# Latent attention: matmuls kept in program order, two key tiles at a time, weight sums in two VectorE accumulators, a quotient by logarithm and exponential

## The chip, the cores and the metric

The kernel runs on 1 core of one Trainium2 chip. The metric is the device time of one execution in microseconds (us), lower is better; the number given is the median of the runs. Engines are named as in the profile: PE is TensorE, PEld its weight loads, DVE is VectorE, ACT is ScalarE, POOL is GpSimd, SP is SyncE, which issues the DMAs.

## What is computed

The reference is a backbone of two layers over 1024 latent tokens and 256 context tokens of width 1024. In each layer the tokens are projected, and three groups of heads mix them: gated linear attention, retention (these two are the "linear heads" below), and multi-head latent attention with 8 heads of 64 value columns. Then come an output projection, layer norms and a convolutional feed-forward block. What the change touches is the latent attention:

```python
def _mla_attend(qn, qr, kn, kr, v):
    s = (jnp.einsum('bqhd,bkhd->bhqk', qn, kn)
         + jnp.einsum('bqhr,bkr->bhqk', qr, kr)).astype(jnp.float32) * MLA_SCALE
    p = jax.nn.softmax(s, axis=-1).astype(v.dtype)
    return jnp.einsum('bhqk,bkhe->bqhe', p, v)
```

Latent tokens attend to all 1280 keys, context tokens (in the first layer alone) to the 256 context keys. All of it is float32; the scores are made of three products of rounded parts (fp32r).

## The kernel before

The kernel is written as Python generators whose steps are woven together, and a tile scheduler then sets each engine's order from the written order and the dependencies; what a generator writes next may so be placed later than another generator's step, or later than its own following step. In each layer `mla` (latent attention) is woven with `lin` (the linear heads, lines 545 to 822), in two stretches of the span; before them lies the input projection (`proj`), behind them `wout` and the feed-forward block.

Latent attention goes head by head. Keys lie on the partitions: for each of 10 key tiles of 128 keys (`kt`) and each half `i` of the 1024 latent queries, `products` (line 942) makes a score tile of 128 keys x 512 queries in a PSUM bank with three fp32r matmuls, and ScalarE writes its exponential to one half of a weight tile of 128x1024 (line 1026, buffer tag `w2`, seven buffers that the projections' split weights use too). Two tiles later `values` (line 948) multiplies: one matmul of 64 columns for each half of the queries, the first into partitions 0 to 63 of the bank "av", the second into 64 to 127, over all ten key tiles. The weights are float32, and a float32 matmul shows as two records in the trace.

The sums of the weights are made elementwise first: GpSimd adds tiles 1 to 6 into tile 0 (line 1037), VectorE tiles 8 and 9 into tile 7 (line 1035), and then tile 7's into tile 0 (line 1043). In the first layer there are also two small tiles for the context queries (line 1013). `quotient` copies the bank "av" away (line 955), sums the accumulator over the keys by a matmul with ones (line 959, again one matmul for each half), takes the reciprocal on VectorE (line 960) and multiplies (line 963). It is a generator too; `tail()` does one step of it.

Beside a head's products the next head is prepared, two steps for each score tile (`beside`): key and query projections (lines 903 and 906, key into partitions 0 to 63 and query into 64 to 127 of the same banks), rotations and values, and `maxima`: one matmul for each block of 128 queries against 512 or 256 keys (line 925) and a maximum over it on VectorE (line 926), through three PSUM banks.

```python
                    elif kt >= 2:
                        k = kt - 2
                        P = held[k]
                        values(h, k, P, 512, k == 9)
                        if k in (8, 9):
                            nc.vector.tensor_tensor(held[7][:], held[7][:], P[:], op=ALU.add)
                        elif 0 < k < 7:
                            nc.gpsimd.tensor_tensor(held[0][:], held[0][:], P[:], op=ALU.add)
```

The linear heads use all engines: in `gla_out` VectorE and GpSimd multiply tiles of 128x512 (lines 693 to 773; line 716 is GpSimd's), `lin_chunk_out` has matmuls of lines 643 and 647, and `lin_norm` ends each group of 256 tokens with two matmuls with a block of ones (lines 660 and 666). Line 195 loads the weights of the dense layers, lines 212 and 213 split them into two parts, line 323 multiplies with them.

## Time and profile before

| | us |
|---|---|
| median of 3 runs | 3635.89 (3632.38 to 3640.07) |
| the profiled execution | 3636.93 |
| its span, first to last instruction | 3635.2 |
| PE busy | 3471.4 |
| DVE busy | 2331.7 |
| ACT busy | 1410.1 |
| POOL busy | 561.8 |

The page gives busy time by engine, the same in 40 slices of the span, the chain of work that ended last, and groups of instructions by line with their busy time, mean length, and the idle time before them with what ended it. A matmul's end is modelled, so how long matmuls take is best read from the start of one row of the timeline to the start of the next. A "PEclk" of 1.00 is TensorE at its full granted clock.

### The profile page before, as it was taken

To read this page: it belongs to the slowest core of one execution; us is meant where nothing else is said; L and a number is where in the kernel's file an instruction comes from. 1 tells how busy PE (TensorE), PEld (TensorE's weight loads), DVE (VectorE), ACT (ScalarE), POOL (GpSimd) and SP (SyncE) were. 2 spreads that over 40 slices of the span, in tenths; PEclk is the share of its full clock that TensorE was granted. 3 is DMA by queue.
4 is the path that set the end of the run, shared out by engine and by line. 5 is a ranking of instruction groups with operands and counts; after the bars stand their busy time and mean duration, and the time that the engine had idled before them with its cause. 6 is when DMAs were issued, how large, how long until landed. Compare 5 with 4: busy or idle time off the path is not lost. (4 is left out here: it accounts for less than half of the span.)

```text
span 3635.2 us, 50748 instructions
## 1 busy us (share of the span) xinstructions
PE 3471.4 (95%) x20270; PEld 2749.7 (76%) x20270; DVE 2331.7 (64%) x3371; ACT 1410.1 (39%) x2355; POOL 561.8 (15%) x583
## 2 busy tenths in 40 slices
PE   8998999997999999999999999889999999999998
PEld 6995544443999999899999897444446788888897
DVE  4336678777676445675557734878776875577555
ACT  3333333333354332343334443333333554345433
POOL 0001454444011000000000000453441000000001
PEclk9998899998999999999999999899999999999999
DMA  8653011021322333432223444011114222323221
GB/s 293 199 175 112 26 31 46 30 82 63 126 72 99 118 118 130 156 103 78 76 76 115 154 132 138 23 35 38 33 48 155 93 93 93 97 90 116 94 95 51
DMA packets 174702, 354.63 MB, mean 98 GB/s; under 512 B 15648, under 2 KB 92912, under 8 KB 174464
## 3 DMA queue, kind: packets, MB, share of 16 engines
q1 hardware_dynamic: 174464, 351.38, 29.5%
q8 instruction: 159, 2.61, 0.3%
q14 instruction: 79, 0.65, 0.1%
HBM read 310.09 MB, written 36.51 MB: 95 GB/s over the span
## 5 line engine op out<-in xcount | busy, mean ns | idle before, releaser
L323 PE MATMUL ps<-h,w 128*128 128x320 f32 (+5 forms) x9600 | 1681.6, 336 | 27.5 <-ACT h L212 16.4
L323 PEld LDWEIGHTS ps<-h,w 128*128 128x128 f32 x9600 | 1539.6, 190 | 166.3 <-ACT h L212 18.7
L213 DVE TENSOR_TENSOR w<-ws,w 128x1024 fp32r<-128x1024 f32 x360 | 440.2, 1223 | 589.7 <-PE ps L323 289.1
L1188 PE MATMUL ps<-hid,w 128*128 128x256 f32 (+4 forms) x3696 | 576.3, 316 | 1.5 <-ACT hid L212 1.5
L1188 PEld LDWEIGHTS ps<-hid,w 128*128 128x128 f32 x3696 | 538.9, 189 | 35.9 <-issue 7.6
L212 ACT CAST w<-ws 128x1024 fp32r<-128x1024 f32 x360 | 379.1, 1054 | 415.4 <-PE ps L1188 290.9
L1026 ACT ACTIVATE w<-ps 128x512 f32<-128x512 f32 x320 | 188.7, 596 | 338.5 <-PE ps L942 332.4
L942 PE MATMUL ps<-h,h 96*128 96x512 f32 (+3 forms) x1008 | 318.7, 431 | 0.3 <-ACT w L1026 0.2
L942 PEld LDWEIGHTS ps<-h,h 96*128 96x128 f32 (+1 forms) x1008 | 183.3, 199 | 151.8 <-issue 92.2
L926 DVE TENSOR_REDUCE sm<-ps 128x1 f32<-128x512 f32 (+1 forms) x400 | 221.7, 585 | 92.2 <-PE ps L925 90.3
L1037 POOL TENSOR_TENSOR w<-w,w 128x1024 f32<-128x1024 f32 x96 | 238.7, 2487 | 271.1 <-PE ps L948 173.0
L948 PE MATMUL ps<-w,hid 128*64 128x512 f32 (+1 forms) x704 | 276.0, 614 | 0.3 <-ACT w L1005 0.3
L1145 POOL MEMSET u<- 128x1 f32 (+1 forms) x264 | 21.5, 103 | 1613.4 <-DVE t L1156 1486.7
L1155 DVE SCALAR_TENSOR_TENSOR t<-u,vec,t 128x642 f32<-128x642 f32 (+3 forms) x176 | 144.6, 822 | 183.8 <-ACT t L1154 183.6
L1149 ACT COPY u<-ps 128x512 f32<-128x512 f32 (+4 forms) x264 | 118.4, 483 | 316.3 <-PE ps L323 316.3
L1193 DVE SCALAR_TENSOR_TENSOR y<-ps,mod,y 128x320 f32<-128x320 f32 (+5 forms) x376 | 197.1, 558 | 68.5 <-PE ps L1188 68.0
L925 PE MATMUL ps<-h,h 96*128 96x512 f32 (+1 forms) x400 | 156.1, 440 | 34.5 <-DVE sm L926 25.3
L925 PEld LDWEIGHTS ps<-h,h 96*128 96x128 f32 x400 | 77.8, 206 | 126.5 <-DVE sm L926 66.6
L716 POOL TENSOR_TENSOR hid<-hid,hid 128x512 f32<-128x512 f32 x108 | 153.3, 1439 | 83.0 <-ACT hid L696 56.2
L1154 ACT ACTIVATE t<-u,vec 128x642 f32<-128x642 f32 (+3 forms) x176 | 153.7, 873 | 0.4
L1156 DVE SCALAR_TENSOR_TENSOR t<-u,vec,t 128x642 f32<-128x642 f32 (+3 forms) x176 | 144.3, 820 | 11.4
L212 ACT CAST hid<-t 128x642 fp32r<-128x642 f32 (+3 forms) x88 | 59.5, 676 | 204.8 <-DVE t L1160 204.8
(197 smaller groups left out, 3134.4 us busy)
## 6 DMA issues: line engine op xcount, KB each, us to landing
ws<-in_up_dram SPq DMA_DIRECT2D x176, 512.0 KB
ws<-in_down_dram SPq DMA_DIRECT2D x88, 512.0 KB
ws<-in_ada_dram SPq DMA_DIRECT2D x80, 512.0 KB
ws<-in_w_in_dram SPq DMA_DIRECT2D x48, 512.0 KB
ws<-in_w_out_dram SPq DMA_DIRECT2D x32, 512.0 KB
y<-in_ada_dram SPq DMA_DIRECT2D x16, 512.0 KB
ws<-in_w_v_dram SPq DMA_DIRECT2D x16, 512.0 KB
hid<-in_xT_dram SPq DMA_DIRECT2D x16, 320.0 KB
```

The lines of the kernel that those rows point to most:

```text
L212: self.nc.scalar.copy(hi, src)
L213: self.nc.vector.tensor_tensor(lo, src, hi.bitcast(F32), op=ALU.subtract)
L323: nc.tensor.matmul(ps[:, i, 0:n], w_[:, k, :], h[k][:, part, o:o + n], start=(k == 0 and q == 0), stop=(k == 7 and q == 2))
L925: nc.tensor.matmul(t, q0[0:96, 128 * qi:128 * qi + 128], k0[0:96, o:o + n], start=True, stop=True)
L926: nc.vector.tensor_reduce(mx[:, qi:qi + 1] if qi < 2 else part[:, qi - 2, j:j + 1], t, axis=AX.X, op=ALU.max)
L942: nc.tensor.matmul(t, Kt[h % 2][ka][0:rows, 128 * kt:128 * kt + 128], Q[h][qa][0:rows, c0:c0 + n], start=(x == 0), stop=(x == 2))
L948: nc.tensor.matmul(op[64 * i:64 * i + 64, 0:n], V[h // 2][kt // 5][:, kt % 5, r:r + 64], P[:, i], start=(kt == 0), stop=last, skip_group_c ...
L1026: nc.scalar.activation(held[kt][:, i], t, AF.Exp, scale=MSCALE)
L1037: nc.gpsimd.tensor_tensor(held[0][:], held[0][:], P[:], op=ALU.add)
L1154: nc.scalar.activation(v[:, 0:n], u[:, 1:1 + n], AF.Identity, scale=cw(j, 1), bias=self.vec[l][:, V_CB + j:V_CB + j + 1])
L1188: nc.tensor.matmul(pb[i][:, 0:n], w[w_][:, x, ms], p.hh[f0 + x][hp][:, o - 1:o - 1 + n], start=(x == 0 and q == 0), stop=(x == gn - 1 and ...
L1193: nc.vector.scalar_tensor_tensor(t, pb[i][:, o:o + n], self.md(l, 5, m, who), t, op0=ALU.mult, op1=ALU.add)
```

## The change

1. A helper `pin` ties every matmul of `mla` to the one written before it, without a semaphore, so that the scheduler keeps them in the order in which they are written. Matmuls of the linear heads may still be placed between them.
2. The loop over key tiles takes two at a time: the products and exponentials of tiles kt and kt+1 (four score tiles), one `tail()`, then the value matmuls of tiles kt-2 and kt-1, both tiles' four matmuls in a row.
3. All adds of weight tiles are on VectorE: tiles 1 to 4 into tile 0, tiles 6 to 9 into tile 5. The two accumulators are not added to each other; `quotient` sums both by matmuls that accumulate in one bank (and both context tiles likewise). GpSimd has no work in `mla` any more but one fill.
4. The reciprocal becomes exp(-ln x) on ScalarE, with a Newton step of two operations on VectorE, whose sign goes into the last multiply.

```diff
+        prev = [None]
+
+        def pin(x):
+
+            if prev[0] is not None:
+                self.tc.add_manual_dep(x.ins, prev[0].ins.name, mybir.DependencyInfo(mybir.DependencyClass.NoSync, mybir.DependencyReason.DATA),
+                                       reason="in order")
+            prev[0] = x
...
-                nc.tensor.matmul(t, Kt[h % 2][ka][0:rows, 128 * kt:128 * kt + 128], Q[h][qa][0:rows, c0:c0 + n], start=(x == 0), stop=(x == 2))
+                pin(nc.tensor.matmul(t, Kt[h % 2][ka][0:rows, 128 * kt:128 * kt + 128], Q[h][qa][0:rows, c0:c0 + n], start=(x == 0), stop=(x == 2)))
...
-        def quotient(h, c0, n, P):
+        def quotient(h, c0, n, sums):
...
             t = bank("pre")[:, 0:n]
+            for x, P in enumerate(sums):
+                for i in range(2):
+                    pin(nc.tensor.matmul(t[64 * i:64 * i + 64, :], self.ones[:, 0:64], P[:, i], start=(x == 0), stop=(x == len(sums) - 1),
+                                         skip_group_check=True))
+            sums.clear()
+            del P
+
+            nc.scalar.activation(rb[:], t, AF.Ln)
+            nc.scalar.activation(rb[:], rb[:], AF.Exp, scale=-1.0)
+            nc.vector.tensor_tensor(u[:], t, rb[:], op=ALU.mult)
+            nc.vector.scalar_tensor_tensor(rb[:], u[:], -2.0, rb[:], op0=ALU.add, op1=ALU.mult)
+            yield
             for i in range(2):
-                nc.tensor.matmul(t[64 * i:64 * i + 64, :], self.ones[:, 0:64], P[:, i], start=True, stop=True, skip_group_check=True)
-            nc.vector.reciprocal(rb[:], t)
-            yield
-            for i in range(2):
-                nc.vector.tensor_tensor(o[r:r + 64, c0 + n * i:c0 + n * i + n], ov[64 * i:64 * i + 64, :], rb[64 * i:64 * i + 64, :], op=ALU.mult)
+                hs = slice(64 * i, 64 * i + 64)
+                nc.vector.scalar_tensor_tensor(o[r:r + 64, c0 + n * i:c0 + n * i + n], ov[hs, :], -1.0, rb[hs, :], op0=ALU.mult, op1=ALU.mult)
...
-            for kt in range(12):
+            for kt in range(0, 12, 2):
                 if kt < 10:
-                    held[kt] = self.w2([128, 2, 512], F32)
...
+                    for k in (kt, kt + 1):
+                        held[k] = self.w2([128, 2, 512], F32)
+                        for i in range(2):
+                            t = bank("sc")
+                            products(h, k, CTX + 512 * i, t)
+                            nc.scalar.activation(held[k][:, i], t, AF.Exp, scale=MSCALE)
+                            beside()
+                            if k == kt or i == 0:
+                                yield
+                tail()
+                if kt >= 2:
+                    for k in (kt - 2, kt - 1):
                         P = held[k]
                         values(h, k, P, 512, k == 9)
-                        if k in (8, 9):
-                            nc.vector.tensor_tensor(held[7][:], held[7][:], P[:], op=ALU.add)
-                        elif 0 < k < 7:
-                            nc.gpsimd.tensor_tensor(held[0][:], held[0][:], P[:], op=ALU.add)
-                        if k not in (0, 7):
-                            del held[k]
+                        if k % 5:
+                            A = held[k // 5 * 5]
+                            nc.vector.tensor_tensor(A[:], A[:], P[:], op=ALU.add)
+                            del held[k], A
                         del P
...
-            nc.vector.tensor_tensor(held[0][:], held[0][:], held[7][:], op=ALU.add)
-            tails.append(quotient(h, CTX, 512, held[0]))
+            tails.append(quotient(h, CTX, 512, [held[0], held[5]]))
```

The order that the scheduler makes of it is seen at three places. The first is PE in the middle of a head of layer 0. Before (L948 are value matmuls, one row a half, L925 row maxima, L942 products):

```order
L948 MATMUL ps<-w_4243,hid_4002 64x512
L925 MATMUL ps<-h_2551,h_4121 128x256
L948 MATMUL ps<-w_4243,hid_4002 64x512
L942 MATMUL ps<-h_3720,h_2549 128x512
L925 MATMUL ps<-h_2551,h_4121 128x512
L942 MATMUL ps<-h_3721,h_2549 128x512
L942 MATMUL ps<-h_3720,h_2550 128x512
```

and now (L957 are value matmuls, L934 row maxima, L951 products, L739 a linear head's):

```order
L934 MATMUL ps<-h_2551,h_4136 128x512
L957 MATMUL ps<-w_4192,hid_4014 64x512 x2
L957 MATMUL ps<-w_4215,hid_4014 64x512 x2
L739 MATMUL ps<-hid_4287,hid_4171 32x128 x2
L951 MATMUL ps<-h_3725,h_2549 128x512
L951 MATMUL ps<-h_3726,h_2549 128x512
L951 MATMUL ps<-h_3725,h_2550 128x512
L934 MATMUL ps<-h_2551,h_4136 128x256
```

The two halves of a key tile, which a row maximum stood between, now stand together, and two tiles' in a row; a product's three matmuls stand together too.

The second is DVE at a quotient of layer 0, with the row maxima around it. Before (L960 the reciprocal, L963 the last multiply, L926 maxima):

```order
L960 RECIPROCAL t_5343<-ps 128x512
L926 TENSOR_REDUCE sm_5421<-ps 128x1
L963 TENSOR_TENSOR y_4951<-t_5342,t_5343 64x512 x2
```

and now (L976 and L977 the Newton step, L981 the last multiply, L935 maxima):

```order
L976 TENSOR_TENSOR t_5388<-ps,t_5387 128x512
L935 TENSOR_REDUCE sm_5471<-ps 128x1
L977 SCALAR_TENSOR_TENSOR t_5387<-t_5388,t_5387 128x512
```

The Newton step's first operation stands where the reciprocal stood, with maxima behind it, and it reads what ScalarE's two steps have made.

The third is PE at the end of layer 0's stretch. Before (L959 the column sums of the last head, L660 and L666 the norm of the last linear group, L323 the output projection):

```order
L660 MATMUL ps<-hid_6386,bones 128x512
L948 MATMUL ps<-w_6427,hid_5654 64x512
L666 MATMUL ps<-hid_6451,bones 128x512
L959 MATMUL ps<-w_6192,ones 64x512 x2
L323 MATMUL ps<-h_6536,w_6492 128x256
```

and now (L969 the column sums, L643 and L647 the last linear group's output):

```order
L969 MATMUL ps<-w_6262,ones 64x512 x2
L969 MATMUL ps<-w_6406,ones 64x512 x2
L643 MATMUL ps<-hid_6451,hid_6503 128x128 x2
L647 MATMUL ps<-hid_6496,u_6448 64x128 x2
...
L660 MATMUL ps<-hid_6458,bones 128x512
L666 MATMUL ps<-hid_6526,bones 128x512
L323 MATMUL ps<-h_6616,w_6572 128x256
```

The last head's sums, which stood behind the last linear group, now stand ahead of that group's end.

Counted over both stretches in these orders, the two programs differ on PE as follows:

| on PE, from the first matmul of attention to its last, both layers | before | now |
|---|---|---|
| value matmuls of 512 queries: pairs of neighbouring halves / with a half of another kind / lone halves | 82 / 3 / 153 | 150 / 1 / 19 |
| key and query projections: pairs and lone halves | 93 | 82 |
| column sums of 512 queries: pairs and lone halves | 19 | 32 |
| neighbours of different tile shape | 782 | 503 |

## Rows read from the trace of the kernel before

**Rows 1.** The page: the span, and PE's busy time, its share and its instructions.

```profile
span 3635.2 us, 50748 instructions
PE 3471.4 (95%) x20270; PEld 2749.7 (76%) x20270; DVE 2331.7 (64%) x3371; ACT 1410.1 (39%) x2355; POOL 561.8 (15%) x583
```

**Rows 2.** Attention stretches: length, busy PE, PEld, DVE, ACT, POOL; PEclk, DMA share, GB/s.

```profile
321.00:902.00 581.00, 521.25 (x2494) 259.61 (x2494) 448.84 (x640) 201.08 (x440) 248.31 (x149) 0.90 0.15 45
2261.00:2760.00 499.00, 458.11 (x2145) 226.76 (x2138) 390.38 (x532) 180.52 (x376) 224.46 (x130) 0.93 0.15 46
```

**Rows 3.** Timeline of PE in layer 0: start us, us, engine, line, operation, records.

```profile
604.17 1.10 PE L942 MATMUL ps<-h,h 96*128 96x512 f32 x4
605.11 0.28 PE L925 MATMUL ps<-h,h 96*128 96x256 f32 x1
605.22 0.39 PE L942 MATMUL ps<-h,h 96*128 96x512 f32 x1
605.54 1.07 PE L948 MATMUL ps<-w,hid 128*64 128x512 f32 x2
606.54 0.50 PE L925 MATMUL ps<-h,h 96*128 96x512 f32 x1
606.98 1.08 PE L948 MATMUL ps<-w,hid 128*64 128x512 f32 x4
607.99 0.51 PE L925 MATMUL ps<-h,h 96*128 96x512 f32 x1
```

**Rows 4.** Timeline of PE, 890 to 893 us.

```profile
890.44 1.93 PE L948 MATMUL ps<-w,hid 128*64 128x512 f32 x6
892.30 0.38 PE L643 MATMUL ps<-hid,hid 128*128 128x128 f32 x1
```

**Rows 5.** Value matmuls by shape: busy us, mean ns, idle before.

```profile
L948 PE MATMUL ps<-w,hid 128*64 128x512 f32 x640 | 267.3, 643 | 0.0
```

**Rows 6.** VectorE's groups, whole span; two by min/median/max ns.

```profile
L1035 DVE TENSOR_TENSOR w<-w,w 128x1024 f32<-128x1024 f32 x32 | 49.0, 1531 | 7.9 <-PE ps L948 7.1 <-issue 0.2
L1043 DVE TENSOR_TENSOR w<-w,w 128x1024 f32<-128x1024 f32 x16 | 20.4, 1276 | 0.2
L1043 DVE TENSOR_TENSOR w<-w,w x16: 1208/1216/2173, 425.0 to 2756.9; 128x1024 f32<-128x1024 f32 x16
L960 DVE RECIPROCAL t<-ps 128x512 f32<-128x512 f32 (+1 forms) x24 | 61.3, 2553 | 7.3 <-PE ps L959 7.1
L963 DVE TENSOR_TENSOR y<-t,t 64x512 f32<-64x512 f32 (+1 forms) x48 | 60.9, 1268 | 0.9
L963 DVE TENSOR_TENSOR y<-t,t x48: 274/690/2831, 376.5 to 2764.4; 64x512 f32<-64x512 f32 x32, 64x128 f32<-64x128 f32 x16
```

**Rows 7.** GpSimd's groups, whole span.

```profile
L1037 POOL TENSOR_TENSOR w<-w,w 128x1024 f32<-128x1024 f32 x96 | 238.7, 2487 | 271.1 <-PE ps L948 173.0 <-ACT w L1026 93.9
L716 POOL TENSOR_TENSOR hid<-hid,hid 128x512 f32<-128x512 f32 x108 | 153.3, 1439 | 83.0 <-ACT hid L696 56.2 <-PE ps L948 9.4 <-DVE hid L338 8.2
```

**Rows 8.** A logarithm or exponential of 128x512 on ScalarE.

```profile
L333 ACT ACTIVATE hid<-hid 128x512 f32<-128x512 f32 x18 | 11.3, 629 | 11.3 <-DVE hid L332 11.0
```

**Rows 9.** Weight loads waiting for maxima, layer 0, layer 1: us, times, longest.

```profile
PEld ps L925 <- DVE sm L926: 39.4, 45, 4.4
...
PEld ps L925 <- DVE sm L926: 27.2, 33, 2.9
```

**Rows 10.** Timeline of PE at the end of layer 0's stretch.

```profile
899.46 1.13 PE L666 MATMUL ps<-hid,bones 128*128 128x512 f32 x2 [2.15 <-ACT hid L663]
900.51 1.08 PE L959 MATMUL ps<-w,ones 128*64 128x512 f32 x4
```

**Rows 11.** Busy us in three short pieces, columns as in rows 2.

```profile
376.00:399.00 23.00, 20.93 (x126) 12.18 (x125) 18.11 (x30) 7.76 (x13) 20.66 (x13) 1.00 0.05 12
399.00:416.00 17.00, 14.35 (x63) 8.21 (x63) 5.99 (x16) 2.43 (x5) 4.76 (x3) 0.51 0.06 17
2280.00:2297.00 17.00, 9.20 (x80) 4.69 (x80) 14.73 (x37) 4.18 (x18) 5.72 (x5) 0.51 0.00 1
```

More of the change, by code (lines that the diff above doesn't have):

```diff
@@ L857, in prod_v @@
             for t_ in range(10):
-                nc.tensor.matmul(ps[:, 128 * t_:128 * t_ + 128], S.ckv[:, 128 * t_:128 * t_ + 128], wk[:, 1, 128 * p:128 * p + 128],
-                                 start=True, stop=True)
+                pin(nc.tensor.matmul(ps[:, 128 * t_:128 * t_ + 128], S.ckv[:, 128 * t_:128 * t_ + 128], wk[:, 1, 128 * p:128 * p + 128],
+                                 start=True, stop=True))
             for i in range(2):
@@ L869, in prod_qr @@
                 for kc in range(2):
-                    nc.tensor.matmul(t, wr[:, kc, 128 * x:128 * x + 128], S.cq[kc][:, o:o + n], start=(kc == 0), stop=(kc == 1))
+                    pin(nc.tensor.matmul(t, wr[:, kc, 128 * x:128 * x + 128], S.cq[kc][:, o:o + n], start=(kc == 0), stop=(kc == 1)))
                 nc.scalar.copy(raw[:, o:o + n].bitcast(F32), t)
@@ L876, in prod_qr @@
                 nc.sync.dma_start(si[:, 0:n], a["msin"][:, o:o + n])
-                nc.tensor.matmul(t, self.permm[:], r, start=True, stop=True)
+                pin(nc.tensor.matmul(t, self.permm[:], r, start=True, stop=True))
                 nc.vector.tensor_tensor(t2[:, 0:n], t, si[:, 0:n], op=ALU.mult)
@@ L924, in maxima @@
                     t = bank("pre")[:, 0:n]
-                    nc.tensor.matmul(t, q0[0:96, 128 * qi:128 * qi + 128], k0[0:96, o:o + n], start=True, stop=True)
+                    pin(nc.tensor.matmul(t, q0[0:96, 128 * qi:128 * qi + 128], k0[0:96, o:o + n], start=True, stop=True))
                     nc.vector.tensor_reduce(mx[:, qi:qi + 1] if qi < 2 else part[:, qi - 2, j:j + 1], t, axis=AX.X, op=ALU.max)
@@ L931, in maxima @@
             t, r = bank("pre"), self.dgt()
-            nc.tensor.matmul(t[0:n, 0:128], mx[:, 10 - n:10], self.ident[:], start=True, stop=True)
+            pin(nc.tensor.matmul(t[0:n, 0:128], mx[:, 10 - n:10], self.ident[:], start=True, stop=True))
             nc.scalar.activation(r[0:n, :], t[0:n, 0:128], AF.Copy, scale=-1.0)
@@ L947, in values @@
             for i in range(2):
-                nc.tensor.matmul(op[64 * i:64 * i + 64, 0:n], V[h // 2][kt // 5][:, kt % 5, r:r + 64], P[:, i], start=(kt == 0), stop=last,
-                                 skip_group_check=True)
-        def quotient(h, c0, n, P):
+                pin(nc.tensor.matmul(op[64 * i:64 * i + 64, 0:n], V[h // 2][kt // 5][:, kt % 5, r:r + 64], P[:, i], start=(kt == 0), stop=last,
+                                 skip_group_check=True))
+        def quotient(h, c0, n, sums):
             r = 64 * (h % 2)
-            o, ov, rb = ob[h // 2], self.tt([128, n]), self.tt([128, n])
+            o, ov, rb, u = ob[h // 2], self.tt([128, n]), self.tt([128, n]), self.tt([128, n])
             nc.scalar.copy(ov[:], self.pb("av")[:, 0:n])
@@ L1012, in mla @@
                     values(h, kt, P[kt], 128, kt == 1)
-                nc.vector.tensor_tensor(P[0][:], P[0][:], P[1][:], op=ALU.add)
-                tails.append(quotient(h, 0, 128, P[0]))
+                tails.append(quotient(h, 0, 128, P))
                 tail()
@@ L1018, in mla @@
             held = {}
-            for kt in range(12):
+            for kt in range(0, 12, 2):
                 if kt < 10:
-                    held[kt] = self.w2([128, 2, 512], F32)
-                for i in range(2):
-                    if kt < 10:
-                        t = bank("sc")
-                        products(h, kt, CTX + 512 * i, t)
-                        nc.scalar.activation(held[kt][:, i], t, AF.Exp, scale=MSCALE)
-                        beside()
-                    if i == 0:
-                        tail()
-                    elif kt >= 2:
-                        k = kt - 2
+                    for k in (kt, kt + 1):
[10 more added lines that the diff above has]
+                    for k in (kt - 2, kt - 1):
                         P = held[k]
                         values(h, k, P, 512, k == 9)
-                        if k in (8, 9):
-                            nc.vector.tensor_tensor(held[7][:], held[7][:], P[:], op=ALU.add)
-                        elif 0 < k < 7:
-                            nc.gpsimd.tensor_tensor(held[0][:], held[0][:], P[:], op=ALU.add)
-                        if k not in (0, 7):
-                            del held[k]
+                        if k % 5:
+                            A = held[k // 5 * 5]
+                            nc.vector.tensor_tensor(A[:], A[:], P[:], op=ALU.add)
+                            del held[k], A
                         del P
-                    if kt < 10:
-                        yield
-            nc.vector.tensor_tensor(held[0][:], held[0][:], held[7][:], op=ALU.add)
-            tails.append(quotient(h, CTX, 512, held[0]))
+                if kt < 10:
+                    yield
+            tails.append(quotient(h, CTX, 512, [held[0], held[5]]))
             tail()
```

7 lines of the change are left out of this document (4 added, 3 removed).

## The prediction

> **What bounds the kernel now.** I read the page first, then the busy times of the two latent-attention stretches, then the timeline of TensorE (PE) inside one, then the groups by line, and the waits last. The profiled execution took 3636.9 us, 1.0 us over the median of the runs (3635.9); its span is 3635.2. PE is busy for 95% of it [rows 1]. The change lives in two stretches, 321 to 902 and 2261 to 2760 us, 1080 us together. There PE is busy for 521.3 and 458.1 us, so 101 us are idle, and its mean granted clock is 0.90 and 0.93; VectorE (DVE) is busy for 448.8 and 390.4, that is 78% [rows 2]. So PE is the limit there, with VectorE close behind.
>
> But PE's busy time is not all needed. The weight-by-value product of a key tile is two matmuls of 64 output columns, one into each half of the partitions (two records each, since the type is fp32). The timeline shows four such records taking from 606.98 to 607.99, **1.01 us, and two records alone from 605.54 to 606.54, 1.00 us** [rows 3]. Two halves that stand next to each other thus run at the same time, and a half by itself costs as much as both. Something between the halves costs the whole second half, and the order of the program before (the first fragment of the change's section) puts a row maximum between them again and again.
>
> **Price of a step and of a change of shape.** I call "step" a pair that runs together, or a lone half. Six records in a row (a pair and a lone half) take from 890.44 to 892.30, 1.86 us [rows 4]; less the 1.00 of the first step, a further step costs 0.86. The first one costs 0.14 more, for leaving. Entering costs too: four products start 0.235 us apart (604.17 to 605.11), but from the last one to the value matmul it is 0.32 (605.22 to 605.54) [rows 3]. In and out cost 0.23, or **0.117 us a change of tile shape**.
>
> **PE, counted in the two orders.**
> - Values of 512 queries: before, 82 pairs, 3 pairs with a key projection, 153 lone halves, 238 steps. After, 151 pairs and 19 lone halves, 170. 68 x 0.86 = -58 us. The group's 267.3 us [rows 5] fit 238 steps of 0.86 to 1.01, with some at the half clock.
> - Key and query projections, now chained in the order written: 93 steps become 82; 11 x 0.86 = -9.
> - Column sums of the weights: each quotient now sums two accumulators, so 19 steps of 512 become 32, +11, and eight more pairs of 128 columns, a quarter each, +2.
> - Changes of shape between neighbours, all matmuls of the stretches counted: 782 become 503; 279 x 0.117 = -33.
>
> Together -87 us at the full clock. The stretches ran at 0.915 on average [rows 2], so **-95 us**. No engine hides this: it is work of the engine that is the limit.
>
> **VectorE.** It gets 128 adds of 128x1024 in place of 32 + 16 and eight of a quarter the size. One line of such adds has a median of 1.22 and a mean of 1.28, the other a mean of 1.53 [rows 6]. At 1.22 the 128 are +156, and those that go are 49.0 + 20.4 + 8 x 0.3 = -72. The reciprocals go, -61. The Newton step adds two operations a quotient: at 0.69 each for the sixteen wide quotients and 0.27 for the eight small (the last multiply's median and shortest, 512 and 128 columns), +26. The last multiply becomes a scalar_tensor_tensor of the same size, 0. Sum: +49. On the other side GpSimd (POOL) loses its 96 adds, 238.7 us [rows 7]. While POOL runs, VectorE slows: the last multiply has a median of 0.69 and a longest of 2.83; at 32 x 0.69 + 16 x 0.27 its 48 would take 26 us instead of 61 [rows 6]. That line alone gives back up to 35, though POOL's other work causes a share. The relief lies between 0 and 239; I take 50, nearest to the row that shows it. VectorE thus stays at about 838 us, in 1013 instead of 1080: 83% in place of 78%.
>
> Against this stands a rule of the Trainium skill (SBUF — State Buffer, Who interferes with whom): a VectorE operation with two SBUF inputs and a GpSimd one that reads SBUF exclude each other, and the loser waits for the whole instruction. By it each of the 80 further adds could wait out a POOL multiply. The trace agrees on the lock only in part: the adds now on VectorE lose 0.3 us on average [rows 6].
>
> In numbers from rows alone: 80 x 0.31 (1.53 less 1.22) is +25 us of VectorE, 80 x 1.44 [rows 7] is +115. I take the first as the bound, since it is the same operation at the same place.
>
> **ScalarE** gets 24 logarithms and 24 exponentials, 0.63 us for a wide one [rows 8], at most 30 us on an engine busy for 35% [rows 2]; the table loads stay as many as they were. They lie in the quotient's chain: VectorE's first multiply now waits for two ScalarE steps (about 1.3 us), with row maxima queued behind it (second fragment), where the reciprocal held the queue for 2.55 on average [rows 6]. I count 0, bounds -1 and +1 us a quotient, 24 us either way. **SyncE** issues the same transfers, in an order that moves only with the quotients. The buffers that hold weights are seven: at a head's start two old accumulators, the last pair and the first new pair fill six, so the third tile's exponentials wait for the old sums. Those stand behind the new head's first products; I count 0, and the cover gone it is one add and one step, 2 us a head.
>
> **What is late next.** PE waits for the row maxima, 39.4 and 27.2 us [rows 9]. With 17% of VectorE's time free instead of 22%, I let these 67 grow in that proportion: **+20 us**. And at the end of layer 0 the third fragment shows the sums ahead of the linear heads' last matmuls. Now this last piece, from its first matmul at 892.30 [rows 4] to the end of the norm's at 900.51 [rows 10], runs beside value matmuls; after, beside nothing: **+8 us**, bounds 0 and 8.
>
> Sum: -95 + 20 + 8 = -67; 3637 - 67 = **3570 us**.
>
> **The rivals.**
> - *The clock comes back as well.* At 0.90 and 0.93 PE loses 58 + 35 = 93 us to half-rate pieces: from 399 to 416 us the clock is 0.51 (the lower of its levels, 1.2 and 2.4 GHz), right behind 23 us at 1.00 in which PE was busy for 20.9 [rows 11]. A third of that gone, and no more waiting than now: 3637 - 95 + 8 - 31 = 3519, with the waiting 3539; say 3530. For it: fewer lone halves. Against: PE will wait on VectorE.
> - *VectorE becomes the limit.* No relief, every add at 1.53: 839 + 49 + 25 = 913 us. In its densest stretch it is busy 14.73 of 17 us, 87% [rows 11]; 913 / 0.87 = 1049, 31 saved, 8 lost: 3614.
> - *Nothing arrives.* The saved PE time falls where PE would wait anyway: 3637.
> - *Slower: adds ahead of maxima.* The 128 adds come in 80 batches, 48 of two. The chain keeps PE from passing a late maximum with a later matmul of attention. If an add isn't covered by the value matmuls issued with it (two pairs, 1.87 us), PE stands for it. 156 us of adds uncovered to three quarters is +117: 3637 - 95 + 8 + 117 = 3667. It decides from 56% uncovered (87 of 156). Against: 1.87 us of matmuls stand beside each batch of 2.44.
> - *Slower: whole waits.* Each of the 80 adds loses 1.44: 839 + 49 + 115 = 1003 us, / 0.87 = 1153, 73 over: 3710. The Trainium skill's rule on the shared port, above, read at its strongest, gives this; the 1.53 of a row speaks against.
>
> **How the numbers follow.** Forecast 0.55, clock 0.13, VectorE 0.18, nothing 0.05, adds ahead of maxima 0.06, whole waits 0.03. A measurement of this kernel can tell 0.2%, 7 us, from no change. Faster: 0.55 + 0.13 + 0.18 = 0.86; same 0.05; slower 0.09. The forecast's own spread is the 24 us of the quotients and the 28 of waiting and end, about 3540 to 3600; the range adds the clock below (3519) and VectorE above (3614): 3518 to 3620.
>
> **What would show it.** Right: the value group falls from 267 us to under 200, and records alone become rare; POOL's adds are gone; the last multiply has a median of 0.69 and a mean near it; the stretches come to about 550 and 465 us. Wrong in a step: PE's waits for maxima grow beyond 90 us; adds on VectorE with means of 1.5 or more; a mean clock under 0.90. The forecast is wrong altogether if pairs stand together in the trace and the stretches are as long as before.

## The result and the profile after

The changed kernel takes **3591.6 us** (median; 3587.6 to 3593.5), the kernel before beside it 3636.1 us. The ratio is 0.9876, with a 95% interval of 0.9859 to 0.9893: 44.6 us faster, where the prediction has 66. The profiled execution took 3592.4 us; the rest is read from it. First the page, for [rows 1]:

```profile
span 3590.7 us, 50954 instructions
...
PE 3398.0 (95%) x20366; PEld 2762.3 (77%) x20366; DVE 2288.0 (64%) x3467; ACT 1433.9 (40%) x2403; POOL 329.3 (9%) x487
```

Then the two attention stretches, with the columns of [rows 2]. The second starts 41 us earlier, since the first is shorter:

```profile
321.00:862.00 541.00, 470.29 (x2537) 260.04 (x2536) 416.88 (x681) 211.34 (x465) 131.98 (x99) 0.88 0.15 46
2220.00:2718.00 498.00, 432.43 (x2135) 236.82 (x2136) 376.73 (x578) 188.44 (x390) 108.58 (x82) 0.86 0.15 46
```

Layer 0 saves 40 us and **layer 1 saves 1**. There PE has 26 us less to do and stands 25 us longer (498.00 less 432.43 is 65.6, against 40.9 in [rows 2]). The granted clock has fallen in both stretches, not risen. VectorE, forecast at 838 us as before, is busy for 794 in the two.

The groups by line, shapes apart, which answer to [rows 5, 6] (L957 values, L1053 all adds, L981 the last multiplication, L976 and L977 the Newton step), and L750, a masked copy of a linear head that the change doesn't touch:

```profile
L957 PE MATMUL ps<-w,hid 128*64 128x512 f32 x640 | 177.1, 648 | 0.0
L1053 DVE TENSOR_TENSOR w<-w,w 128x1024 f32<-128x1024 f32 x128 | 176.8, 1382 | 24.2 <-PE ps L957 18.4 <-ACT w L1042 3.7
L981 DVE SCALAR_TENSOR_TENSOR y<-t,t 64x512 f32<-64x512 f32 x32 | 23.9, 746 | 0.5
L750 DVE COPY_PREDICATED t<-msk,hid 32x128 f32<-32x128 uint8 x72 | 21.3, 295 | 1.0
L977 DVE SCALAR_TENSOR_TENSOR t<-t,t 128x512 f32<-128x512 f32 x16 | 11.0, 688 | 0.1
L976 DVE TENSOR_TENSOR t<-ps,t 128x512 f32<-128x512 f32 x16 | 11.0, 687 | 10.3 <-PE ps L951 7.1 <-ACT t L975 3.1
```

The value group falls from 267.3 to 177.1 us: the pairs are there. The masked copies fall from 636 to 295 ns on average without having been changed. In the kernel before they were (mean; then shortest, median and longest):

```profile
L750 DVE COPY_PREDICATED t<-msk,hid 32x128 f32<-32x128 uint8 x72 | 45.8, 636 | 0.9
L750 DVE COPY_PREDICATED t<-msk,hid x72: 281/298/2422, 392.7 to 2702.4; 32x128 f32<-32x128 uint8 x72
```

Most of them were as short then as now; some stood for up to 2.1 us, nearly one add of GpSimd (2.49 us in [rows 7]). Now the longest takes 305 ns.

What PE waited for from 320 to 2830 us, both stretches within (us in total, times, longest). First the longest in the kernel before, the maxima; then the changed kernel. The maxima (L934 on L935) are one of several now; the transpose of a head's maxima (L941), the sums (L969) and the first maxima of a head (L934 on L922) are new at this size:

```profile
PE ps L925 <- DVE sm L926: 25.3, 22, 4.2
...
PE ps L934 <- DVE sm L935: 26.5, 22, 5.5
PE ps L941 <- DVE sm L937: 25.9, 12, 5.3
PE ps L969 <- DVE h L922: 16.4, 4, 8.6
PE ps L934 <- DVE h L922: 10.5, 6, 2.9
```

The longest of these, on the timeline of PE (start us, us, then the operation):

```profile
686.91 2.31 PE L915 MATMUL ps<-y,ws 128*64 128x512 f32 x7
689.15 1.08 PE L727 MATMUL ps<-hid,hid 128*32 128x256 f32 x24
698.86 3.68 PE L969 MATMUL ps<-w,ones 128*64 128x512 f32 x8 [8.63 <-DVE h L922]
```

and what VectorE does meanwhile:

```profile
687.16 2.06 DVE L1053 TENSOR_TENSOR w<-w,w 128x1024 f32<-128x1024 f32 x1
689.14 1.50 DVE L758 TENSOR_TENSOR hid<-u 128x256 f32<-128x256 f32 x1
690.56 2.28 DVE L1053 TENSOR_TENSOR w<-w,w 128x1024 f32<-128x1024 f32 x1
692.76 1.48 DVE L761 TENSOR_TENSOR hid<-hid,u 128x256 f32<-128x256 f32 x1
694.17 1.21 DVE L1053 TENSOR_TENSOR w<-w,w 128x1024 f32<-128x1024 f32 x1
695.30 1.54 DVE L922 TENSOR_TENSOR h<-ps,h 64x1024 fp32r<-64x1024 f32 x2
...
697.58 1.57 DVE L922 TENSOR_TENSOR h<-ps,h 64x1024 fp32r<-64x1024 f32 x2
```

K and Q of the next head have just been multiplied (L915). The sums need a bank that the subtractions (L922) must empty first, and these stand behind three adds of weights and two steps of a linear head. Two of the adds take 2.06 and 2.28 us, the third 1.21, in a stretch in which GpSimd works for the linear heads (3.92 of the first 4 us, 3.96 of the next 9, below). In the chain nothing of attention may pass the sums. So PE stands for 8.63 us, and starts again at a lower clock (third piece; columns of [rows 2]):

```profile
686.00:690.00 4.00, 4.00 (x38) 1.79 (x34) 4.00 (x3) 0.56 (x2) 3.92 (x3) 1.00 0.04 11
690.00:699.00 9.00, 0.36 (x12) 0.14 (x4) 8.92 (x10) 3.39 (x6) 3.96 (x3) 0.72 0.00 0
699.00:715.00 16.00, 15.86 (x85) 9.47 (x86) 13.35 (x27) 9.29 (x23) 7.63 (x7) 0.84 0.07 18
```

### The profile page after: what moved, and what is told of

It reads as the page before. It is cut to its first block, busy times and chain, and to the rows that moved or that the text cites. A ratio compares the mean times of both kernels' runs of the same rounds, so it can differ in the third digit from the quotient of the medians.

```text
span 3590.7 us, 50954 instructions
## 1 busy us (share of the span) xinstructions
PE 3398.0 (95%) x20366; PEld 2762.3 (77%) x20366; DVE 2288.0 (64%) x3467; ACT 1433.9 (40%) x2403; POOL 329.3 (9%) x487
## 5 line engine op out<-in xcount | busy, mean ns | idle before, releaser
L323 PE MATMUL ps<-h,w 128*128 128x320 f32 (+5 forms) x9600 | 1676.0, 335 | 21.4 <-ACT h L212 12.6
L323 PEld LDWEIGHTS ps<-h,w 128*128 128x128 f32 x9600 | 1535.5, 190 | 158.3 <-ACT h L212 14.8
L951 PE MATMUL ps<-h,h 96*128 96x512 f32 (+3 forms) x1008 | 317.3, 436 | 3.8 <-DMA h<-mx 2.3
L951 PEld LDWEIGHTS ps<-h,h 96*128 96x128 f32 (+1 forms) x1008 | 189.5, 205 | 107.9 <-issue 70.2
L935 DVE TENSOR_REDUCE sm<-ps 128x1 f32<-128x512 f32 (+1 forms) x400 | 222.9, 588 | 52.3 <-PE ps L934 50.2
L934 PE MATMUL ps<-h,h 96*128 96x512 f32 (+1 forms) x400 | 153.3, 442 | 50.5 <-DVE sm L935 26.5
L1053 DVE TENSOR_TENSOR w<-w,w 128x1024 f32<-128x1024 f32 x128 | 176.8, 1382 | 24.2 <-PE ps L957 18.4
L957 PE MATMUL ps<-w,hid 128*64 128x512 f32 (+1 forms) x704 | 183.7, 618 | 0.0
L716 POOL TENSOR_TENSOR hid<-hid,hid 128x512 f32<-128x512 f32 x108 | 160.6, 1505 | 137.9 <-ACT hid L696 75.3
L934 PEld LDWEIGHTS ps<-h,h 96*128 96x128 f32 x400 | 84.2, 217 | 99.9 <-DVE sm L935 48.9
```

What stands on the lines that cost most here:

```text
L323: nc.tensor.matmul(ps[:, i, 0:n], w_[:, k, :], h[k][:, part, o:o + n], start=(k == 0 and q == 0), stop=(k == 7 and q == 2))
L716: nc.gpsimd.tensor_tensor(X[n][:], blk(E[n][:, 0, cs[i]]), qx[:], op=ALU.mult)
L934: pin(nc.tensor.matmul(t, q0[0:96, 128 * qi:128 * qi + 128], k0[0:96, o:o + n], start=True, stop=True))
L935: nc.vector.tensor_reduce(mx[:, qi:qi + 1] if qi < 2 else part[:, qi - 2, j:j + 1], t, axis=AX.X, op=ALU.max)
L951: pin(nc.tensor.matmul(t, Kt[h % 2][ka][0:rows, 128 * kt:128 * kt + 128], Q[h][qa][0:rows, c0:c0 + n], start=(x == 0), stop=(x == 2)))
L957: pin(nc.tensor.matmul(op[64 * i:64 * i + 64, 0:n], V[h // 2][kt // 5][:, kt % 5, r:r + 64], P[:, i], start=(kt == 0), stop=last, skip_gro ...
```

## The experiments

One table first. Steps (of the wide value matmuls) and changes of shape are counted in each order as ahead of the prediction. The four columns behind them are the two stretches together, from the row of the stretches: PE busy, PE idle (length less busy), VectorE busy, and what the clock loses (one less the granted clock, times the length). The column "time" is the median of the runs, and the last one its difference from the kernel before as timed beside it. The change was timed beside 3636 us, all others beside 3631 to 3632; so a difference from the change comes out some 4 us apart by the two columns (the text below takes the times).

| kernel | steps | shape changes | PE busy | PE idle | VectorE | clock | time | against before |
|---|---|---|---|---|---|---|---|---|
| before | 238 | 782 | 979 | 101 | 839 | 93 | 3636 | |
| the change | 170 | 503 | 903 | 136 | 794 | 135 | 3592 | -45 |
| before + chain | 173 | 583 | 947 | 193 | 841 | 182 | 3693 | +60 |
| before + pairs, no chain | 160 | 645 | 925 | 123 | 840 | 137 | 3617 | -15 |
| before + quotient | 230 | 763 | 975 | 99 | 816 | 110 | 3624 | -6 |
| before + adds | 242 | 789 | 964 | 59 | 817 | 67 | 3584 | -47 |
| before + adds + quotient | 242 | 789 | 957 | 51 | 793 | 61 | 3561 | -70 |
| before + adds + quotient + two tiles (the change, no chain) | 219 | 662 | 920 | 51 | 786 | 64 | 3523 | -109 |
| the change, no chain, pairs | 160 | 585 | 850 | 68 | 797 | 57 | **3467** | -165 |
| the change, half the adds on GpSimd | 172 | 512 | 916 | 171 | 804 | 153 | 3640 | +8 |
| the change, reciprocal | 171 | 492 | 922 | 155 | 830 | 148 | 3635 | +3 |
| the change, maxima out of the chain | 200 | 580 | 916 | 104 | 792 | 107 | 3571 | -60 |
| the change, spaced | 173 | 495 | 871 | 109 | 781 | 89 | 3537 | -95 |
| the change, no chain, pairs, answers first | 160 | 566 | 874 | 96 | 815 | 83 | 3527 | -106 |

**The chain alone, and all but the chain.** Theory A is the prediction's: the chain's order removes work from PE, and that is the gain. Rival B: the gain is what VectorE gets back, and the chain only costs. First the chain on the kernel before (and on every other matmul of its attention):

```diff
-                nc.tensor.matmul(t, q0[0:96, ...], k0[0:96, o:o + n], start=True, stop=True)
+                pin(nc.tensor.matmul(t, q0[0:96, ...], k0[0:96, o:o + n], start=True, stop=True))
```

> The kernel before with only the chain over attention's matmuls. In its order the value matmuls take 173 steps (238 before, 170 in the change) and 583 changes of tile shape (782, 503). Theory A, the gain is PE time of halves that now run together: 65 steps of 0.86 and 199 shape changes of 0.117 are about -80 us, less what the chain costs in waits and clock (about 40 in the change): 3585 to 3605 us. Rival B, the gain is VectorE's and GpSimd's (adds off GpSimd, no reciprocal) and the pairs are hidden: 3630 to 3660 us, since the chain alone can only add waits.

Measured: 3692.5 us, 1.0165 times the kernel before (1.0148 to 1.0181). The stretches and PE's longest waits there:

```profile
321.00:923.00 602.00, 499.73 (x2490) 270.63 (x2489) 437.00 (x636) 200.42 (x438) 252.10 (x149) 0.84 0.14 42
2281.00:2819.00 538.00, 447.68 (x2125) 240.27 (x2126) 403.60 (x532) 182.40 (x377) 223.78 (x130) 0.84 0.13 42
```

```profile
PE ps L934 <- DVE sm L935: 55.8, 30, 8.9
PE ps L968 <- DVE h L922: 34.2, 10, 6.9
```

PE is busy for 32 us less and idle for 92 more, most of it on VectorE's answers. Then the reverse: the changed kernel, its `pin` empty.

```diff
         def pin(x):
-            if prev[0] is not None:
-                self.tc.add_manual_dep(x.ins, prev[0].ins.name, ...)
             prev[0] = x
```

> The changed kernel without the chain: two key tiles at a time, adds on VectorE and the new quotient stay. In its order 219 steps for the values, 662 changes of shape. Theory A: 19 steps and 120 shape changes fewer than before, 16 more steps for the sums, about -17 us, and no strict order to wait for: 3610 to 3625 us. Rival B: as fast as the change or faster, 3575 to 3595 us.

Measured: 3523.2 us, ratio 0.9697 (0.9680 to 0.9715).

```profile
321.00:843.00 522.00, 493.68 (x2554) 258.63 (x2552) 416.89 (x683) 208.28 (x468) 131.75 (x101) 0.92 0.16 49
2199.00:2648.00 449.00, 426.76 (x2135) 222.16 (x2134) 369.34 (x576) 186.99 (x387) 104.98 (x82) 0.95 0.16 50
```

So the chain costs the change 68 us, net of the steps that it saves. Without it PE does 18 us more (920 for 903) and stands for 51 us instead of 136. Theory A falls for the chain; the rest of the change is worth more than B expected.

**Parts put back into the change.** The adds of key tiles 1 to 4 back on GpSimd, then the reciprocal back on VectorE:

```diff
-                            nc.vector.tensor_tensor(A[:], A[:], P[:], op=ALU.add)
+                            (nc.gpsimd if k < 5 else nc.vector).tensor_tensor(A[:], A[:], P[:], op=ALU.add)
```

> The changed kernel with the adds of key tiles 1 to 4 on GpSimd (64 of 128). VectorE loses 64 x 1.38 = 88 us of work and gets the slowdown under GpSimd back (some 45 us for 64 adds). Theory A: PE's steps are the same (172), so within 10 us of the change: 3582 to 3602 us. Rival B: the adds on GpSimd cost, 3605 to 3625 us.

```diff
-            nc.scalar.activation(rb[:], t, AF.Ln)
-            nc.scalar.activation(rb[:], rb[:], AF.Exp, scale=-1.0)
-            nc.vector.tensor_tensor(u[:], t, rb[:], op=ALU.mult)
-            nc.vector.scalar_tensor_tensor(rb[:], u[:], -2.0, rb[:], op0=ALU.add, op1=ALU.mult)
+            nc.vector.reciprocal(rb[:], t)
...
```

> The changed kernel with VectorE's reciprocal in place of logarithm, exponential and Newton step. VectorE gets 61 us of reciprocals for 26 us of Newton steps, 35 us more in all, at 24 places. Theory A: PE's steps are the same (171); between 3588 and 3605 us. Rival B: all 35 us show, 3620 to 3630 us.

Measured: 3640.2 us (ratio to before 1.0020, 1.0008 to 1.0032) and 3634.8 us (0.9999, 0.9983 to 1.0014). Each alone takes the whole gain back. In the first VectorE is busy for 11 us more, though 64 adds (88 us) have left it, and 49 us are lost; in the second it is busy for 36 us more, and 43 are lost: little more than VectorE's time. In the first, VectorE's groups and GpSimd's adds by line and shape:

```profile
L750 DVE COPY_PREDICATED t<-msk,hid 32x128 f32<-32x128 uint8 x72 | 47.6, 661 | 1.0
L981 DVE SCALAR_TENSOR_TENSOR y<-t,t 64x512 f32<-64x512 f32 x32 | 37.2, 1162 | 0.6
...
L1053 POOL TENSOR_TENSOR w<-w,w 128x1024 f32<-128x1024 f32 x64 | 161.5, 2523 | 339.2 <-PE ps L957 285.3 <-ACT hid L333 32.0 <-issue 18.2
```

64 adds on GpSimd bring the masked copies from 295 back to 661 ns and the last multiplications from 746 to 1162: the relief that the prediction called 50 us is real, and most of it is lost with half of the adds.

**Parts added to the kernel before.** Theory C, formed of the first four runs: PE's work is not what limits; VectorE's late answers are. Rival D: the loop over two key tiles gives the gain by its order. Adds alone (the change's own lines for them, and both accumulators summed), quotient alone, both:

```diff
-                        if k in (8, 9):
-                            nc.vector.tensor_tensor(held[7][:], held[7][:], P[:], op=ALU.add)
-                        elif 0 < k < 7:
-                            nc.gpsimd.tensor_tensor(held[0][:], held[0][:], P[:], op=ALU.add)
+                        if k % 5:
+                            A = held[k // 5 * 5]
+                            nc.vector.tensor_tensor(A[:], A[:], P[:], op=ALU.add)
...
```

> The kernel before with one part of the change: all adds of the weights on VectorE into two accumulators (and both summed by TensorE); the reciprocal stays, one key tile at a time, no chain. Theory C: TensorE stands for VectorE's answers, and half of the gain of 113 us that the change without its chain has over the kernel before comes from GpSimd leaving the memory that it shares with VectorE; VectorE's own work rises by 12 us a layer or so, but the reciprocal, the multiplications and the copies get back to their undisturbed times. 3565 to 3595, with TensorE's idle time in the two attention stretches down by 10 to 25 us each. Rival D: the gain is the order that the loop over two key tiles makes; then this kernel takes 3620 to 3650, since TensorE's order is that of the kernel before (242 steps of the value matmuls against 238) and VectorE has no less to do.

> The kernel before with one part of the change: the quotient by Ln and Exp on ScalarE and a Newton step on VectorE in place of the reciprocal; the adds stay on GpSimd and VectorE as before. Theory C: 16 reciprocals of 3.3 us (with their share of disturbed ones) leave VectorE's queue and 32 short instructions of some 0.7 us take their place; as in the run that put the reciprocal back, that is worth a little more than VectorE's time alone: 3585 to 3610. Rival D: 3620 to 3640, since the order on TensorE hardly changes (230 steps against 238).

> The kernel before with both of these parts, that is, the change without its chain and without its loop over two key tiles at a time. Theory C: nearly all that the change without its chain gains, 3520 to 3545; the two parts together give about the sum of what they give alone. Rival D: the loop over two key tiles gives most; then 3590 to 3620.

Measured: adds 3584.4 us (0.9871, 0.9856 to 0.9885); quotient 3624.5 (0.9974, 0.9964 to 0.9983); both 3561.5 (0.9807, 0.9792 to 0.9821). The stretches of the adds alone:

```profile
321.00:866.00 545.00, 511.83 (x2536) 256.47 (x2534) 433.67 (x665) 196.39 (x435) 131.65 (x99) 0.93 0.15 46
2230.00:2708.00 478.00, 451.91 (x2136) 224.04 (x2137) 383.32 (x569) 178.72 (x374) 108.27 (x82) 0.94 0.15 47
```

VectorE takes 80 more wide adds and is busy for 22 us *less* than before; PE's idle time falls from 101 to 59 us, and the clock loses 26 us less. This is what C said, but for the reciprocal: it took 3354 ns before and takes 3353 now, so it had not been slowed. Nor had TensorE or ScalarE stood for GpSimd's adds themselves: among the waits of the kernel before there is none on L1037. What the second accumulator gives by itself was not tried; it came with the adds. The quotient fell short of it (6 us alone, 23 behind the adds). The stretches of both:

```profile
320.00:853.00 533.00, 503.61 (x2555) 257.70 (x2554) 420.11 (x683) 210.18 (x469) 134.53 (x101) 0.93 0.16 49
2210.00:2685.00 475.00, 452.90 (x2139) 221.65 (x2136) 372.61 (x576) 186.09 (x387) 105.81 (x82) 0.95 0.15 47
```

Of the 109 us some 39 are still missing after both: they come with the loop over two key tiles, by which PE is busy for 36 us less (957 to 920) while its idle time stays. At the prediction's prices the 23 steps and 127 changes of shape between these two orders are 35 us. So D holds for that part, and C's "PE's work does not limit" can't be right once the adds are off GpSimd.

**The maxima out of the chain**, with their transpose:

```diff
-                    pin(nc.tensor.matmul(t, q0[0:96, ...], k0[0:96, o:o + n], start=True, stop=True))
+                    nc.tensor.matmul(t, q0[0:96, ...], k0[0:96, o:o + n], start=True, stop=True)
...
-            pin(nc.tensor.matmul(t[0:n, 0:128], mx[:, 10 - n:10], self.ident[:], start=True, stop=True))
+            nc.tensor.matmul(t[0:n, 0:128], mx[:, 10 - n:10], self.ident[:], start=True, stop=True)
```

> The changed kernel with the matmuls of the row maxima, and the transpose of these, taken out of the chain; every other matmul of the attention stays in it (200 steps of the value matmuls, 580 changes of shape). Theory C: it is the maxima's transpose and their rotating banks, for which the chained TensorE stands, and both are free now: the waits on the final reduction (14 us in the second layer's stretch) and most of those on the maxima's reductions go, and the time falls to 3530 to 3555. Rival D: the chain costs by what it holds back at the changes of heads as a whole (K and Q copies, V, the sums), and it matters little whether the maxima are in it: 3575 to 3595.

Measured: 3570.5 us (0.9833, 0.9818 to 0.9849), between the two. PE's wait on the last reduction stays, at 19.9 us for 25.9; the maxima are a quarter to a third of the chain's cost and not its core.

**Pairs without the chain.** The runs so far had pairing and chain together. A higher priority for the second matmul of a pair parts them:

```diff
             for i in range(2):
-                nc.tensor.matmul(op[64 * i:64 * i + 64, 0:n], V[h // 2][kt // 5][:, kt % 5, r:r + 64], P[:, i], ...)
+                with self.tc.high_priority() if i else ExitStack():
+                    nc.tensor.matmul(op[64 * i:64 * i + 64, 0:n], V[h // 2][kt // 5][:, kt % 5, r:r + 64], P[:, i], ...)
```

On the kernel before, and nothing else:

> The kernel before with one thing changed: the second of the two value matmuls of a key tile gets a higher priority than all else in TensorE's order, so that all 160 pairs of 512 columns run together (160 steps against 238, 645 changes of shape against 782); no chain, nothing else of the change. This parts the pairing from the chain, which the run with the chain alone had together. Theory E (the price of TensorE's work in the prediction was right, and the chain took it back by making TensorE stand): 78 steps at 0.86 us and 137 changes at 0.117 us are 83 us: 3545 to 3580. Theory C (TensorE's matmul work is not what limits this kernel, VectorE's late answers are; the work that is saved turns into idle time): 3605 to 3640.

On the changed kernel without its chain (there also for the sums, and for Q beside K):

> The changed kernel without its chain; in its place a higher priority for the second matmul of each value pair and each pair of sums, and for the matmuls of Q beside those of K (160 steps of the value matmuls against 219, 585 changes of shape against 662). Theory E: 59 steps at 0.86 us and 77 changes at 0.117 us off the 3523 of the change without its chain: 3450 to 3480, the fastest kernel of the study. Theory C: 3505 to 3530, with TensorE's idle time in the two attention stretches up by what its busy time loses.

Measured: 3616.6 us on the kernel before (0.9951, 0.9932 to 0.9969), and 3467.3 on the other (0.9541, 0.9521 to 0.9560). The stretches of the first:

```profile
322.00:885.00 563.00, 490.27 (x2490) 257.95 (x2489) 452.95 (x638) 199.75 (x438) 247.35 (x149) 0.86 0.15 46
2245.00:2730.00 485.00, 434.67 (x2131) 228.35 (x2123) 387.33 (x531) 179.73 (x375) 222.39 (x130) 0.88 0.15 46
```

and of the second:

```profile
318.00:814.00 496.00, 452.15 (x2556) 248.56 (x2554) 422.23 (x686) 208.95 (x468) 132.15 (x101) 0.92 0.17 53
2170.00:2592.00 422.00, 397.40 (x2168) 216.50 (x2168) 374.48 (x580) 188.82 (x391) 111.14 (x82) 0.96 0.18 56
```

On the kernel before, pairing takes 54 us from PE's busy time, of which 22 turn up as idle time, and the clock loses 44 us more: 15 remain by the medians (32 in the stretches of the profiled execution, which ended nine under its median). On the other kernel the priority takes 71 from PE, 18 turn up as idle time, the clock loses 8 less, and **56 remain**. C and E are both right, each for one of the two kernels. Between the two stand the adds, the quotient, the two tiles at a time and the wider priority; which of them lets the pairs pay was not run apart. The last kernel is the fastest of the study, 124 us under the change.

**The change, with room in its chain.** For each head but the first, five empty places between its K and Q and the first maximum, three ahead of the transpose:

```diff
             yield
+            if h:
+                for _ in range(5):
+                    yield
 
         def maxima(h):
...
             yield
+            if h:
+                for _ in range(3):
+                    yield
             n = 10 - lo // 128
```

> The changed kernel, chain and all, with eight empty places put into the chained order for each head but the first: five between the K and Q of a head and its first row maximum, three between the last row maximum and the transpose of the maxima, so that products and values stand there and VectorE has time for its copies and its last reduction (173 steps, 495 changes of shape). If the chain costs by these two places (theory C's places: 39 us of waits of the transpose, the sums and the first maxima in the changed kernel), 3555 to 3575. If it costs by each wait for a bank of the row maxima all along the head, 3585 to 3600.

Measured: 3536.6 us (0.9730, 0.9715 to 0.9745), 55 under the change. PE's waits in both stretches (L947 the transpose, L975 the sums, L937 the maxima):

```profile
PE ps L937 <- DVE sm L938: 37.8, 31, 5.6
PE ps L975 <- DVE h L922: 18.0, 5, 7.8
PE ps L947 <- DVE sm L940: 8.7, 3, 5.3
```

The transpose's wait falls from 25.9 to 8.7 us, that of the first maxima on K and Q goes from 10.5 to 4.1; the sums' doesn't move, and the maxima's own grows. PE is idle for 27 us less, and busy for 32 less, as the clock loses 46 less. So most of the chain's net cost goes when the written order leaves room at two places; against the pairs without a chain, 69 us are still missing. The gain is larger than the expectation had it; what the clock gives back, it had not counted.

**Answers first.** On the fastest kernel, a higher priority on VectorE for the maxima's reductions and for the subtractions of K and Q:

```diff
-                    nc.vector.tensor_reduce(mx[:, qi:qi + 1] if qi < 2 else part[:, qi - 2, j:j + 1], t, ...)
+                    with self.tc.high_priority():
+                        nc.vector.tensor_reduce(mx[:, qi:qi + 1] if qi < 2 else part[:, qi - 2, j:j + 1], t, ...)
...
```

> The kernel of the run before (all but the chain, pairs by priority, 3467 us), and on VectorE the row maxima's reductions, their last reduction and the subtractions that finish K and Q get a higher priority than the adds of the weights and all else (160 steps, 566 changes of shape). It asks whether what is left of TensorE's waits on VectorE comes of the order on VectorE, adds ahead of maxima. If so, a third to two thirds of the 33 us that TensorE's waits on the maxima and on K and Q take there go: 3440 to 3457. If VectorE serves them in turn already and is only too busy, 3460 to 3475.

Measured: 3526.9 us (0.9712, 0.9699 to 0.9726), 60 us slower than without it, outside both expectations. The waits on the maxima fall (15.1 to 10.6 us), and a linear head's matmuls take their place at the top:

```profile
PE ps L727 <- DVE hid L703: 20.8, 13, 3.5
```

In the kernel without the edit this wait was 4.1 us. In the stretches TensorE stands for 27 us longer, is busy for 25 longer while the clock loses 27 more, and VectorE is busy for 18 longer. The 16.7 us more of this one wait are thus a part of the 60; how far the rest follows from the new order on VectorE was not tried.

## Why the prediction was right, and which steps were not

The time lies in the range, on the side that was likeliest, at two thirds of the forecast gain. The stretches were forecast at about 550 and 465 us and took 541 and 498: the second saved nothing. The sum and its causes are two things here.

- **PE, -95: by size nearly right, its condition wrong.** PE's busy time in the stretches falls by 77 us. The clock loses 42 us more than before, and part of PE's busy time is that loss. Where the clock hardly moves, the prices hold: between the change without chain and the same with pairs stand 66 steps (59 of values, 4 of K and Q, 3 of sums) at 0.86 and 77 changes of shape at 0.117, 66 us, or 70 at a clock of 0.94; the rows show 71. That this meets so closely is partly chance: by the matmuls that start together in the two traces it is 57 steps of values, 16 of K and Q (some of them shorter) and 8 of sums, up to 79 us, or 84. So the prices hold within a sixth. The step that failed is "No engine hides this: it is work of the engine that is the limit". The pairs alone give 15 us on the kernel before, and 56 on the kernel with the other three parts (with the priority for sums and Q beside them); the chain that was to bring them costs 60 by itself.
- **VectorE, 0: the step that failed most.** "VectorE thus stays at about 838 us" came out at 794. The adds cost 1.38 and not 1.22, 177 us for 156. But the relief, put at 50 between 0 and 239, comes out at 115: 839 + 177 - 72 - 61 + 26 is 909, and 794 were measured. The prediction sized it by one line, the last multiplication, and that line does give back 32 of its "up to 35". Line by line (mean before less mean now, times their number, in the stretches) 74 us more come back at operations that it did not read, nearly all of the linear heads, and all with their inputs in SBUF alone; those that read a PSUM bank give back nothing. With the adds alone moved the same count is 110, the last multiplication included, and again nothing at PSUM. And it was no side account: moving the adds alone gives 47 us, the largest gain of the parts that were added alone to the kernel before (two tiles alone was not run). The Trainium skill's rule (SBUF — State Buffer, Who interferes with whom) was weighed as a price for 80 new adds. It cuts the other way too: GpSimd's 96 adds were what VectorE's other operations ran into. The masked copies (636 to 295 to 661 ns as the adds leave GpSimd and half of them come back) agree with it: the longest take 2422, 305 and 2444 ns, and L743, the same operation on 128x128 with one input in PSUM, takes 296, 295 and 296 on average. So "the trace agrees on the lock only in part" took a mean for the lock, which met few operations and held those for nearly a whole add.
- **The quotient, 0 within 24 us either way.** Alone 6 us, behind the adds 23, and in the chain 43: beyond the bound. That it weighs more there because PE stands for VectorE's queue is a reading of the waits, and not shown apart.
- **Two key tiles at a time.** Never a term of its own; it was in the counted order. Behind adds and quotient it is worth 39 us without any chain.
- **Waits, +20, and the end of layer 0, +8.** Idle time rises by 36 us for the 28 forecast, but not at the maxima: these waits of PE's weight loads, 39.4 and 27.2 in [rows 9], fell to 32.0 and 16.9. And a weight load's wait overlaps matmuls: PE itself stood for the maxima for 25.3 us before, not 67, and for 26.5 now. The new waits are on the last reduction and on K and Q, which the prediction did not look at. At the end of layer 0 the sums do stand ahead (859 us), and the last linear group runs from 861.57 to 867.89 beside nothing: 6.3 us.
- **The rivals.** The clock did not come back; it went from 0.90 and 0.93 to 0.88 and 0.86, one of the signs named for a step being wrong. VectorE is no limit by its share, 76%. "Adds ahead of maxima" named the right mechanism at the wrong place: the chain does keep PE from passing a late answer behind the adds, at K and Q's subtractions (the 8.63 us above). Its price, 68 us for the whole chain, was more than paid by the parts put at zero. Whole waits did not come: the adds' mean of 1.38 is under the 1.53 of [rows 6].

So the forecast came out near in part by luck, by errors that cancel: the chain counted as a gain, and the move of the adds and the quotient counted as nothing. Built up one on the other, by the last column of the table, the adds give 47 us, the quotient 23, the two tiles 39, and the chain takes back 64: 45. What is open: how far the clock is the cause of the differences and how far it follows from the standing; it moves with the idle time in nearly every row of the table, and no run here changed it by itself.

## What to carry over

Work that is taken from the busiest engine is worth its price only while the others answer in time: ask which engine it waits for, and what slows that one, before the count. A strict order turns every late answer into a stand of the whole engine; to bring two instructions together, a priority for the second is enough and leaves the rest free to pass. When a change has several parts, measure them both alone and on top of each other: the pairs were worth 15 us alone and 56 on a kernel with three other parts.

## What had not been expected of the hardware

- A masked copy of 32x128 on VectorE, with its inputs in SBUF, takes 295 ns, and on average 636 to 661 with GpSimd's adds in the program, as a few of the 72 stand for up to 2.1 us (2422 ns at the longest, a GpSimd add takes 2487). The same operation on 128x128 with an input in PSUM stays at 296. An add of 128x1024 loses less in proportion: 1.21 us undisturbed, 1.53 and 1.28 on average beside GpSimd's adds [rows 6]. Moving 80 such adds *to* VectorE made it less busy, by 22 us.
- A reciprocal of 128x512 takes 3.35 us on VectorE. Logarithm, exponential and the two Newton operations take 0.60, 0.63, 0.69 and 0.69: shorter also in a row. The reciprocal in the kernel before, then the logarithm and the exponential in the changed one:

```profile
L960 DVE RECIPROCAL t<-ps 128x512 f32<-128x512 f32 x16 | 53.7, 3354 | 6.3 <-PE ps L959 6.1
...
L974 ACT ACTIVATE t<-ps 128x512 f32<-128x512 f32 x16 | 9.5, 596 | 36.2 <-PE ps L969 34.5 <-DVE sm L935 1.6
L975 ACT ACTIVATE t<-t 128x512 f32<-128x512 f32 x16 | 10.1, 632 | 0.4
```
